# An embedding lookup on one core: the first indices move to a second issuing engine, and the second half of the positions moves ahead of the raw indices

## The chip, the cores and the metric

The kernel runs on one core of one Trainium2 chip. The metric is the time of one execution on the device, in microseconds (us), as the median of several runs. A second number appears in the profiles: the span, from the first to the last recorded instruction of one profiled execution. The span is some microseconds shorter than the device time.

The engines that matter here are GpSimd (POOL in the profile), which issues the gathers; VectorE (DVE), which adds the positions; ScalarE (ACT), which in the kernel before issues every plain transfer and computes nothing; and SyncE (SP), which in the kernel before issues nothing. The transfers themselves are moved by 16 DMA engines that all issuing engines share. A `q` after an engine's name in the profile (ACTq, POOLq) marks what the engine's sequencer did: issue, wait, drain.

## The reference

```python
batch, seq_len, vocab_size, d_model = 32, 512, 50000, 512
token_embed = embedding_table[indices]          # 32 x 512 rows of 2 KB
return (token_embed + position_embed).astype(np.float32)
```

So 16384 rows of 2 KB (33.55 MB) are read from a table of 50000 rows at random places, a row of positions is added to each, and 33.55 MB are written. The positions are 1 MB in all, and the indices reach the kernel as 64-bit words.

## The kernel before

A position s of the sequence is written as s = 4p + k: p is one of 128 partitions, k runs from 0 to 3. One gather takes 128 rows, those of one batch entry b and one k, so that there are 32 x 4 = 128 gathers of 256 KB, numbered g in the order in which they are issued. For the first four batch entries the order takes k = 0 and 1 of all four entries first, and then k = 2 and 3.

There are four kinds of loads. `idx0` holds the indices of the first four batch entries, fetched in the layout that the gathers need: entry 0 by itself (4 KB in pieces of 32 bytes), entries 1 to 3 after it (12 KB). `idx_raw` holds all indices as they lie in memory, in four loads of 32 KB, and one transpose on VectorE makes `idx_t` of them for the other 28 entries. The positions come in two halves of 512 KB: half 0 is for k = 0 and 1, half 1 for k = 2 and 3.

```python
    def load(out, in_, done):
        return nc.scalar.dma_start(out=out, in_=in_).then_inc(done, 16)      # L95

    def load_pos(h):
        part = slice(h * half, (h + 1) * half)
        return load(pos_sb[:, part, :], pos_rows[:, part, :], s_pos[h])

    # two loads ahead of the barrier with which the framework closes
    for ins in (load(idx0[:, 0, :], idx_first[:, 0, :], s_first), load_pos(0)):
        tc.no_tile_sem_insts.add(ins.ins.name)
    tc.close()                       # the profile gives the barriers to L106
    tc.compile()

    # the rest of the loads, behind the barrier
    load(idx0[:, 1:, :], idx_first[:, 1:, :], s_next)
    for j in range(J):               # J = 4
        load(idx_raw[j * B : (j + 1) * B, :], idx_rows[:, j, :], s_raw)
    load_pos(1)
```

GpSimd issues the gathers. It waits for entry 0's indices, for the next three entries' ahead of the third gather, and for the transpose ahead of the seventeenth:

```python
    nc.gpsimd.wait_ge(s_first, 16)
    for g, (b, k) in enumerate(order):
        if g == half:                # half = 2
            nc.gpsimd.wait_ge(s_next, 16)
        if g == FIRST * K:           # 16
            nc.gpsimd.wait_ge(s_idx, 1)
        # ... (a wait for stores, once, where the slots are reused)
        ins = nc.gpsimd.indirect_dma_start(                                  # L128
            out=slots[b % SLOTS][:, k, :], out_offset=None, in_=table,
            in_offset=bass.IndirectOffsetOnAxis(ap=where, axis=0),
        ).then_inc(s_gather[g % LANES], 16)
        if g >= LANES:               # 10 gathers may be under way
            ins._wait_ge(s_gather[g % LANES], rounds(g - LANES))
```

VectorE copies each quarter of the positions into PSUM when the first batch entry needs it, adds, and makes the transpose ahead of the eighth add:

```python
    for g, (b, k) in enumerate(order):
        if g == 7:
            nc.vector.transpose(out=idx_t[:], in_=...)._wait_ge(s_raw, 16 * J).then_inc(s_idx, 1)  # L140
        if b == 0:
            nc.vector.tensor_copy(out=pos_ps[:, k, :], in_=pos_sb[:, k, :])._wait_ge(              # L145
                s_pos[k // half], 16).then_inc(s_ps, 1)
            nc.vector.wait_ge(s_ps, k + 1)
        part = slots[b % SLOTS][:, k, :]
        nc.vector.tensor_tensor(out=part, in0=part, in1=pos_ps[:, k, :], op=add                    # L150
            )._wait_ge(s_gather[g % LANES], rounds(g)).then_inc(s_add, 1)
```

ScalarE then issues 68 stores (60 of 512 KB, 8 of 256 KB; L159), each as soon as the adds it needs are done. The last store's landing ends the kernel.

Of the kernel before, what the change touches and what calls it, by code (L numbers as in the profile page):

```python
# [1 line left out]

# [4 lines left out]

P = 128
K = 4
SLOTS = 23  # L10
LANES = 10
FIRST = 4
Q = 32


@with_exitstack
def kernel(
    ctx: ExitStack,
    tc: tile.TileContext,
    indices: bass.AP,  # L20
    embedding_table: bass.AP,
    position_embed: bass.AP,
    out: bass.AP,
):

    nc = tc.nc
    f32 = mybir.dt.float32
    i32 = mybir.dt.int32
    add = mybir.AluOpType.add

    B, S = indices.shape
    V, D = embedding_table.shape
    assert S == P * K and B == 32
    J = P // Q  # L40
    assert B == Q, "indices are turned in squares of 32"


    idx_words = indices.bitcast(i32)
    idx_first = idx_words[0:FIRST].rearrange("b (p w) -> p b w", p=P)
    idx_rows = idx_words.rearrange("b (j w) -> b j w", j=J)
    out_rows = out.rearrange("b (p k) d -> b p k d", k=K)
    pos_rows = position_embed.rearrange("(p k) d -> p k d", k=K)
    table = embedding_table[:, :]

    def sbuf(name, shape, dtype):
        return nc.alloc_sbuf_tensor(name, shape, dtype).ap()

    idx0 = sbuf("idx0", [P, FIRST, 2 * K], i32)
    idx_raw = sbuf("idx_raw", [P, 2 * Q * K], i32)
    idx_t = sbuf("idx_t", [P, K, B], i32)
    pos_sb = sbuf("pos_sb", [P, K, D], f32)
    slots = [sbuf(f"slot{n}", [P, K, D], f32) for n in range(SLOTS)]
    pos_ps = nc.alloc_psum_tensor("pos_ps", [P, K, D], f32).ap()

    half = K // 2
    order = [(b, k) for h in range(2) for b in range(FIRST)
             for k in range(h * half, (h + 1) * half)]
    order += [(b, k) for b in range(FIRST, B) for k in range(K)]
    stores = []
    for g, (b, k) in enumerate(order):
        if (b <= 1 and k < half) or b == B - 1:
            stores.append((g + 1, b, k, 1))  # L70
        elif k % half == half - 1:
            stores.append((g + 1, b, k + 1 - half, half))

    sems = []

    def sem(name):
        sems.append(nc.alloc_semaphore(name))
        return sems[-1]

    s_first, s_next, s_raw = sem("s_first"), sem("s_next"), sem("s_raw")  # L80
    s_pos = [sem(f"s_pos{h}") for h in range(2)]
    s_gather = [sem(f"s_gather{n}") for n in range(LANES)]

    reused = range(B - SLOTS)
    s_out, s_idx, s_ps = sem("s_out"), sem("s_idx"), sem("s_ps")
    s_add, s_rest, s_pool = sem("s_add"), sem("s_rest"), sem("s_pool")
    nums = [x.num for x in sems]
    assert nums == list(range(nums[0], nums[0] + len(nums)))
    early, late = range(nums[0], nums[-3]), range(nums[-3], nums[-1] + 1)

    def rounds(g):
        return 16 * (g // LANES + 1)

    def load(out, in_, done):
        return nc.scalar.dma_start(out=out, in_=in_).then_inc(done, 16)  # L95

    def load_pos(h):
        part = slice(h * half, (h + 1) * half)
        return load(pos_sb[:, part, :], pos_rows[:, part, :], s_pos[h])

    for ins in (load(idx0[:, 0, :], idx_first[:, 0, :], s_first), load_pos(0)):
        tc.no_tile_sem_insts.add(ins.ins.name)
    tc.close()
    tc.compile()  # L106


    load(idx0[:, 1:, :], idx_first[:, 1:, :], s_next)
    for j in range(J):  # L110
        load(idx_raw[j * B : (j + 1) * B, :], idx_rows[:, j, :], s_raw)
    load_pos(1)


    nc.gpsimd.wait_ge(s_first, 16)
    for g, (b, k) in enumerate(order):
        if g == half:
            nc.gpsimd.wait_ge(s_next, 16)
        if g == FIRST * K:
            nc.gpsimd.wait_ge(s_idx, 1)  # L120
        if b == SLOTS and k == 0:
            done = sum(1 for x in stores if x[1] in reused)
            nc.gpsimd.wait_ge(s_out, 16 * done)  # L123
        if b < FIRST:
            where = idx0[:, b, 2 * k : 2 * k + 1]
        else:
            where = idx_t[:, k, b : b + 1]
        ins = nc.gpsimd.indirect_dma_start(  # L128
            out=slots[b % SLOTS][:, k, :],
            out_offset=None,  # L130
            in_=table,
            in_offset=bass.IndirectOffsetOnAxis(ap=where, axis=0),
        ).then_inc(s_gather[g % LANES], 16)
        if g >= LANES:
# [5 lines that stand above are left out]
            nc.vector.transpose(  # L140
                out=idx_t[:],
                in_=idx_raw[:].rearrange("r (q k w) -> r k q w", k=K, w=2)[:, :, :, 0],
            )._wait_ge(s_raw, 16 * J).then_inc(s_idx, 1)
        if b == 0:
            nc.vector.tensor_copy(out=pos_ps[:, k, :], in_=pos_sb[:, k, :])._wait_ge(  # L145
                s_pos[k // half], 16
            ).then_inc(s_ps, 1)
            nc.vector.wait_ge(s_ps, k + 1)
        part = slots[b % SLOTS][:, k, :]
        nc.vector.tensor_tensor(  # L150
            out=part, in0=part, in1=pos_ps[:, k, :], op=add
        )._wait_ge(s_gather[g % LANES], rounds(g)).then_inc(s_add, 1)


    rest = 0
    for adds, b, at, n in stores:
        done = s_out if b in reused else s_rest
        rest += b not in reused
        nc.scalar.dma_start(  # L159
            out=out_rows[b][:, at : at + n, :],  # L160
            in_=slots[b % SLOTS][:, at : at + n, :],
        )._wait_ge(s_add, adds).then_inc(done, 16)

    nc.gpsimd.wait_ge(s_add, len(order))
    nc.gpsimd.drain()
    nc.gpsimd.dma_reset(early)
    nc.gpsimd.sem_clear(early).then_inc(s_pool, 1)
    nc.scalar.wait_ge(s_pool, 1)  # L170
    nc.scalar.wait_ge(s_rest, 16 * rest)
    nc.scalar.sem_clear(late)

# [1 line left out]
_INS = ['indices', 'embedding_table', 'position_embed']  # L175
_OUTS = [((32, 512, 512), 'float32')]


# [23 lines left out]
```

## Time and profile before

| | |
|---|---|
| device time, median of 3 runs | 179.27 us (178.99 to 179.32) |
| span of the profiled execution | 173.3 us |
| bytes moved in the span | 68.34 MB, 394 GB/s on average |
| VectorE busy | 90.7 us (52%) |
| GpSimd busy | 121.4 us (70%) |

The page of the profile also cuts the span into 40 slices of 4.3 us and gives, for each, the busy share of the 16 DMA engines and the rate. The rate is 128 and 242 GB/s in the first two slices, between 324 and 392 in the next five, and above 400 from the eighth slice to the last but one. A part of the page lists groups of instructions with their mean duration, and the idle time of the engine ahead of them with the name of what ended it; "issue" there means that the engine waited for nothing that the profile shows. A packet is a piece of a transfer that one DMA engine moves at a time. The trace has a record of each packet: its queue, size, start and duration. Queue q0 carries the gathers, and q10 carries everything that ScalarE issues.

### The profile page before, as it was taken

The page shows a single profiled execution, that of the slowest core. Times are in us where ns is not written, and L with a number is a line of the kernel's source. Part 1 is how long each engine was busy: PE and PEld are TensorE (multiplying, and loading weights), DVE is VectorE, ACT ScalarE, POOL GpSimd, SP SyncE. Part 2 cuts the span into 40 slices and gives each one's busy share as a digit, 9 for nine tenths or more (in the row PEclk, how much of TensorE's full clock was granted, in tenths as well). Part 3 has the DMA queues.
Part 4 walks back from the last instruction along what each step waited for, and adds up shares of the span by engine and source line. Part 5 has one row for each costly group of instructions (what it writes and reads, how often), then busy time and mean ns, then how long its engine had stood idle before and what let it go on. Part 6 is the DMA issues. An engine that isn't in the chain of part 4 may idle for free.

```text
span 173.3 us, 387 instructions
## 1 busy us (share of the span) xinstructions
DVE 90.7 (52%) x133; POOL 121.4 (70%) x132
## 2 busy tenths in 40 slices
DVE  0433855545555554555555555545555555546551
POOL 2777777777777777777777777777777777777400
DMA  4899999999999999999999999999999999999997
GB/s 128 242 324 331 345 392 365 415 409 412 411 415 402 407 421 419 409 421 420 420 416 421 420 417 419 422 416 420 421 419 417 421 419 418 419 422 415 420 420 308
DMA packets 21059, 68.34 MB, mean 394 GB/s; under 512 B 3776, under 2 KB 3904, under 8 KB 21056
## 3 DMA queue, kind: packets, MB, share of 16 engines
q10 hardware_dynamic: 10816, 34.76, 49.8%
q0 software_dynamic: 10240, 33.56, 49.7%
q14 instruction: 3, 0.02, 0.0%
HBM read 34.75 MB, written 33.55 MB: 394 GB/s over the span
## 4 chain that ended last, share of the span: by engine, by line
POOL 68%; issue 23%; DMA 5%; DVE 1%; POOLq 0%
POOL slot L128 68%; DMA slot<-in_embedding_table_dram,idx_t 4%; DVE slot L150 1%; DMA idx<-in_indices_dram 1%; POOLq L123 0%
## 5 line engine op out<-in xcount | busy, mean ns | idle before, releaser
L128 POOL DMA_INDIRECT slot<-in_embedding_table_dram,idx_t x112 | 105.9, 946 | 34.1 <-issue 34.1
L150 DVE TENSOR_TENSOR slot<-slot,pos_ps 128x512 f32<-128x512 f32 x128 | 87.9, 687 | 74.9 <-issue 46.1
L128 POOL DMA_INDIRECT slot<-in_embedding_table_dram,idx x16 | 15.3, 954 | 7.3 <-issue 4.6
L145 DVE COPY pos_ps<-pos_sb 128x512 f32<-128x512 f32 x4 | 2.8, 688 | 4.6 <-DMA pos_sb<-in_position_embed_dram 4.6
L140 DVE STREAM_TRANSPOSE idx_t<-idx_raw 128x128 int32<-128x128 int32 x1 | 0.4, 399 | 0.0
L186 POOL MEMSET const-float32-0.0<- 128x1 f32 x1 | 0.1, 98 | 0.2 <-issue 0.2
L186 POOL MEMSET const-uint8-127<- 128x1 uint8 x1 | 0.1, 118 | 0.0
L186 POOL MEMSET const-bfloat16-1.0<- 128x1 bf16 x1 | 0.1, 113 | 0.0
L186 POOL MEMSET const-float32-1.0<- 128x1 f32 x1 | 0.1, 104 | 0.0
## 6 DMA issues: line engine op xcount, KB each, us to landing
out_dram<-slot ACTq DMA_DIRECT2D x60, 512.0 KB
out_dram<-slot ACTq DMA_DIRECT2D x8, 256.0 KB
slot<-in_embedding_table_dram,idx_t POOLq DMA_INDIRECT x112
pos_sb<-in_position_embed_dram ACTq DMA_DIRECT2D x2, 512.0 KB, 4.6
slot<-in_embedding_table_dram,idx POOLq DMA_INDIRECT x16
idx_raw<-in_indices_dram ACTq DMA_DIRECT2D x4, 32.0 KB
idx<-in_indices_dram ACTq DMA_DIRECT2D x1, 4.0 KB, 1.6
idx<-in_indices_dram ACTq DMA_DIRECT2D x1, 12.0 KB
```

Of the source, the lines that this page charges most:

```text
L128: ins = nc.gpsimd.indirect_dma_start(out=slots[b % SLOTS][:, k, :], out_offset=None, in_=table, in_offset=bass.IndirectOffsetOnAxis(ap=whe ...
L140: nc.vector.transpose(out=idx_t[:], in_=idx_raw[:].rearrange("r (q k w) -> r k q w", k=K, w=2)[:, :, :, 0],)._wait_ge(s_raw, 16 * J).then_ ...
L145: nc.vector.tensor_copy(out=pos_ps[:, k, :], in_=pos_sb[:, k, :])._wait_ge(s_pos[k // half], 16).then_inc(s_ps, 1)
L150: nc.vector.tensor_tensor(out=part, in0=part, in1=pos_ps[:, k, :], op=add)._wait_ge(s_gather[g % LANES], rounds(g)).then_inc(s_add, 1)
L186: nc = _bacc.Bacc("TRN2", target_bir_lowering=False, num_devices=1)
```

## The change

The load of entry 0's indices is issued by SyncE, so that ScalarE can issue the first half of the positions at once, beside it. Behind the barrier, the second half of the positions is issued ahead of the four loads of raw indices and no longer behind them. The intent is to start the positions' two transfers earlier, in a stretch where few transfers are under way. No transfer is added or removed, and no wait of GpSimd, VectorE or of the stores is changed.

```diff
-    def load(out, in_, done):
-        return nc.scalar.dma_start(out=out, in_=in_).then_inc(done, 16)
+    def load(out, in_, done, engine=nc.scalar):
+        return engine.dma_start(out=out, in_=in_).then_inc(done, 16)
@@
-    for ins in (load(idx0[:, 0, :], idx_first[:, 0, :], s_first), load_pos(0)):
+    for ins in (
+        load(idx0[:, 0, :], idx_first[:, 0, :], s_first, engine=nc.sync),
+        load_pos(0),
+    ):
         tc.no_tile_sem_insts.add(ins.ins.name)
     tc.close()
     tc.compile()
 
     load(idx0[:, 1:, :], idx_first[:, 1:, :], s_next)
+    load_pos(1)
     for j in range(J):
         load(idx_raw[j * B : (j + 1) * B, :], idx_rows[:, j, :], s_raw)
-    load_pos(1)
```

## The prediction

> **What bounds the kernel now.** I read the chain of waits first, for what sets the end; then busy time in stretches, to see whether the DMA engines have room; then the timeline of the first 8 us, where the whole change lies; then the instructions of the barrier's line. The chain in order of time, cut to its first 8 us:
>
> ```profile
> 0.68 0.06 issue
> 0.74 1.60 DMA idx<-in_indices_dram
> 2.33 0.80 issue
> 3.13 1.08 POOL slot L128
> 4.21 0.31 issue
> 4.51 0.94 POOL slot L128
> 5.46 0.30 issue
> 5.76 0.95 POOL slot L128
> ```
>
> The columns are start, length and what it was. The chain is the load of entry 0's indices (1.60 us from issue to landing), 0.80 us in which nothing is named, and then gathers at a strict distance of 1.25 us (4.51, 5.76). The last of the 128 is issued at 162.06, and (162.06 - 4.51)/126 = 1.2504 us confirms that none was ever held up: 10 gathers may be under way, and the group of idle times says "issue" for 127 of 128. So GpSimd is a metronome, and the end is its start plus 127 x 1.25 plus the delay of the last gather, add and store. But the DMA engines are full too:
>
> ```profile
> 2.00:4.00 2.00, 0.00 (x0) 0.87 (x1) 1.00 0.78 257
> 4.00:5.00 1.00, 0.36 (x1) 0.69 (x2) 1.00 0.66 112
> 5.00:6.00 1.00, 0.34 (x1) 0.70 (x2) 1.00 0.78 230
> 6.00:8.00 2.00, 1.19 (x2) 1.65 (x2) 1.00 0.94 286
> ...
> 15.00:20.00 5.00, 2.98 (x6) 3.78 (x5) 1.00 1.00 360
> ...
> 100.00:160.00 60.00, 32.79 (x48) 45.37 (x49) 1.00 1.03 419
> 160.00:169.00 9.00, 5.01 (x8) 2.40 (x3) 1.00 1.03 419
> ```
>
> The last two columns are the share of the DMA engines and GB/s. From 6 us on the share is near 1. GpSimd asks for one gather and, later, one equal store in each 1.25 us: 2 x 262144 B / 1.2504 us = 419 GB/s, which is just what the engines move between 100 and 160 us, and also between 160 and 169, when GpSimd has stopped asking (its last issue ends at 163.0). Demand and capacity are therefore equal within what I can read. The backlog tells the same: from a gather's issue to its add the first takes 6.81 - 3.13 = 3.7 us, the last 169.54 - 162.06 = 7.5 us. What matters at the end is a sum of three: when gathers start, how much backlog the first 30 us leave, and the tail after the last gather's landing (173.3 - 169.5 = 3.8 us).
>
> What ends the wait of GpSimd at 3.13 is the point in doubt. The timeline of the loads and the barrier's line:
>
> ```profile
> 0.74 0.38 ACTq L95 DMA_DIRECT2D idx<-in_indices_dram  x1
> 1.15 0.46 ACTq L95 DMA_DIRECT2D pos_sb<-in_position_embed_dram  x1
> 2.36 0.39 ACTq L95 DMA_DIRECT2D idx<-in_indices_dram  x1
> 2.78 1.93 ACTq L95 DMA_DIRECT2D idx_raw<-in_indices_dram  x4
> 4.73 0.45 ACTq L95 DMA_DIRECT2D pos_sb<-in_position_embed_dram  x1
> ```
> ```profile
> L106 POOLq EVENT_SEMAPHORE  x4: 17/17/17, 1.8 to 2.2; - x4
> L106 ACTq DRAIN  x2: 8/80/151, 1.6 to 2.0; - x2
> ```
>
> ScalarE ends its second issue at 1.61, drains for 0.15 us, and only then does GpSimd's semaphore step of the barrier run (1.8); the other engines had drained by 0.8. ScalarE is the last to arrive, so its two issues set the barrier. GpSimd leaves it at 2.23 + 0.02 = 2.25; the indices land at 2.33. Two candidates thus lie 0.08 us apart, and either could be what the 0.80 us follow.
>
> [...] The trace puts that issue time at 0.38 to 0.46 us each[...]. [...] No two plain rings are at work together in the trace before, so it shows nothing of SyncE's; where gathers and raw indices overlap (5 to 6.4 us) the packet records show the 1 KB packets strewn among the gathers' 4 KB packets up to 6.37[...]. [...]
>
> **The change part by part.**
>
> Part one, the indices on SyncE. It takes one issue, 0.41 us (1.15 - 0.74), from ScalarE ahead of the barrier. SyncE is ready when ScalarE is: both leave the earlier barrier at 0.66 and SyncE's first drain of L106 is at 0.7. The best case: both issue at about 0.74, the indices land at 2.33 as before, half 0 of the positions starts 0.41 earlier, the barrier opens at 1.84 and everything that ScalarE issues behind it moves up 0.41. If the 0.80 us follow the barrier, the first gather still can't be ahead of the landing at 2.33 but may start near 2.72 (3.13 - 0.41). If they follow the landing, it stays at 3.13.
>
> The cost of part one is company. In the kernel before, the 128 packets of 32 B (7 to 9 ns each) run alone, from 1.73 to 1.99 by the packet records, and the positions' first 4 KB packet starts at 2.24. That is 0.99 and 1.09 us after their issues. With both issued at 0.74 the positions' packets begin at 1.83, within the indices' 0.26 us. Each DMA engine has 8 index packets; some 3 are through by 1.83 (8 x 0.10/0.26), and if the other 5 have to take turns with 4 KB packets of 160 to 500 ns each, they end 5 x 0.2 = 1.0 us later. [...] I weigh: no delay 45%, about half a microsecond 35%, near one microsecond 20%. Of the gain of 0.41 I take half, and of a delay that falls on GpSimd's start I count all: 0.5 x -0.41 x 0.45 + 0.35 x 0.45 + 0.2 x 0.9 = +0.25 us as a mean, with a median at 0 to +0.1.
>
> Part two, half 1 of the positions ahead of the raw indices. Its issue moves from 4.73 to about 2.37 (2.78 - 0.41), and the four raw loads from 2.78 to about 2.83, almost where they were. Nobody waits for either: the copy of quarter 2 runs at 19.2, and the transpose that reads the raw indices at 18.15, with no idle time ahead of it; its result is first used at 23.27. So no wait is removed. What changes is which packets fill the stretch from 4 to 6 us. There the engines move 0.112 + 0.230 = 0.34 MB; with 512 KB of positions in the queue they can move as much as in the stretches beside it, 257 to 286 GB/s, 0.54 MB in two microseconds. That takes 0.20 MB out of the full stretch, worth 0.20 MB / 419 GB/s = 0.48 us of backlog. The second gather and the ones after it lose the half load in front of them (the second took 10.28 - 4.51 = 5.8 us to its add); the first one gets it instead, and may land about half a microsecond later (4 of its packets on each engine, each behind one of 160 ns: 0.6 us). Moving everything of ScalarE up by 0.41 fills more of the same holes, up to another 0.2 us.
>
> How much of the 0.48 to 0.7 survives for 160 us is a choice. If capacity truly equals demand, a backlog that is smaller at 30 us is smaller at the end, and all of it counts. If instead the rate rises with the backlog (360 GB/s at 15 to 20 us, 419 later), the queue refills to the same level and none of it counts. I take 60%, -0.36 us.
>
> Sum: +0.05 (median of part one) - 0.36 = -0.3, so 179.27 - 0.3 = 179.0; the chance that the barrier is what GpSimd follows pulls a little further: 178.9 us.
>
> **The rivals.** First, the metronome alone: the end follows GpSimd's start and nothing else. For it speaks that no gather was held up. Then the time is 179.27 minus 0.41 if the barrier frees GpSimd (178.9), unchanged if the landing does, and up to 180.2 if the indices are slowed by 0.9 in company. Second, the DMA engines alone: GpSimd's start is of no matter, all work filled into holes counts. For it speaks the share of 1.03 after GpSimd has stopped, at 419 GB/s. Then 0.5 to 1.1 us are won: 178.2 to 178.8. Third, a second plain ring costs time that lies outside the span, at the program's start or end (179.27 against 173.3 us of span leaves 6 us that no view shows); nothing here speaks for or against it, and I allow half a microsecond.
>
> **Range and chances.** The extremes are -1.3 (the gains of both in full) and +1.0 (indices late, backlog refills); 8 times in 10 it should lie between 177.9 and 179.9. Two per cent are 3.6 us, more than all that the change touches in the first 6 us. I give 0.02 to faster by over 2%, 0.96 to within 2%, 0.02 to slower.
>
> **What would show it.** In the changed kernel's trace: ScalarE's first issue is the positions' at 0.74 and its next at about 1.95; SyncE's issue stands at 0.73 to 0.74, and its landing at 2.33 says that company is free, [...]at 3.2 or later that packets took turns. The first gather at 2.72 says barrier, at 3.13 landing. The stretch from 4 to 6 us should show 250 GB/s or more. The last gather's delay to its add, 7.5 us before, should be near 7.1 if the emptier queue survives, and 7.5 if it refills. The prediction is wrong if the indices land after 3.5, if the metronome of 1.25 us breaks because the next three entries' indices come late (needed at 5.76), or if the time moves by over 1 us with a span that doesn't.

## The result, and the profile after

The changed kernel took 177.92 us (median of 4 runs, 177.83 to 178.63) against 179.29 us before (4 runs): a ratio of 0.9936 with a 95% interval of 0.9908 to 0.9964. The span of the profiled execution hardly moved: 173.2 us after, 173.3 us before. So of the 1.37 us won in time, 0.1 us stands in the profile. One number on record bears on this at once: the execution of the kernel before whose span was 173.3 us took 177.92 us itself, which is the changed kernel's median. The kernel before thus stands on record at 177.92 us and at 178.99 to 179.32 us, without the change. That contradiction is the first thing to settle.

The chain of waits of the changed kernel, in order of time (start, length, what):

```profile
0.68 0.07 issue
0.74 2.08 DMA idx<-in_indices_dram
2.82 0.27 issue
3.09 1.08 POOL slot L131
4.17 0.30 issue
4.48 0.95 POOL slot L131
```

The load of the first indices now takes 2.08 us to land, 0.48 us more than before (1.60). But the unnamed stretch behind it shrank from 0.80 to 0.27 us, so that the first gather starts at 3.09, 0.04 us earlier than before. An "issue" piece that changes its length when its supposed cause moves was not caused by it. The barrier's line tells what was:

```profile
L109 POOLq EVENT_SEMAPHORE  x4: 17/17/17, 1.4 to 1.8; - x4
L109 ACTq DRAIN  x2: 8/80/153, 1.2 to 1.6; - x2
```

GpSimd's last step of the barrier moved from 2.2 to 1.8 (in the trace it ends at 2.25 before and at 1.79 after), behind a drain of ScalarE that starts 0.47 us earlier. The timeline of the loads shows why:

```profile
0.74 0.40 ACTq L95 DMA_DIRECT2D pos_sb<-in_position_embed_dram  x1
0.74 0.37 SPq L95 DMA_DIRECT2D idx<-in_indices_dram  x1
1.90 0.39 ACTq L95 DMA_DIRECT2D idx<-in_indices_dram  x1
2.32 0.51 ACTq L95 DMA_DIRECT2D pos_sb<-in_position_embed_dram  x1
2.86 1.87 ACTq L95 DMA_DIRECT2D idx_raw<-in_indices_dram  x4
```

Both engines issue at 0.74, and neither issue is longer than it was before (0.46 and 0.38). Last, the stretches (busy times, then the last two columns: share of the DMA engines, GB/s):

```profile
4.00:5.00 1.00, 0.69 (x1) 0.69 (x2) 1.00 0.79 242
5.00:6.00 1.00, 0.00 (x0) 0.70 (x2) 1.00 0.84 245
...
10.00:15.00 5.00, 2.41 (x4) 3.78 (x5) 1.00 0.85 245
15.00:20.00 5.00, 2.48 (x5) 3.78 (x5) 1.00 1.01 360
...
100.00:160.00 60.00, 32.79 (x48) 45.37 (x49) 1.00 1.03 419
```

and one stretch of the kernel before:

```profile
10.00:15.00 5.00, 2.70 (x5) 3.78 (x5) 1.00 0.99 346
```

The hole from 4 to 6 us is filled as intended: 242 and 245 GB/s where there were 112 and 230. But a new hole follows it: from 10 to 15 us the engines carry 245 GB/s where they carried 346. By the packet records the changed kernel is 0.23 MB ahead at 6 us, level at 12 us and 0.18 MB behind at 15 us. Nearly all that is missing from 10 to 15 us is gathers (0.64 against 1.11 MB; stores 0.59 against 0.61), and their 4 KB packets took 277 ns each on average, against 195 before and 159 from 100 to 105 us in both kernels. Why the packets take longer there isn't shown. So nothing is left at 15 us, and the last gather takes 169.62 - 162.02 = 7.6 us from issue to add, against 7.5 us before.

### The profile page after: what moved, and what is told of

Read it like the earlier page. It is cut to its first block, busy times and chain, and to the rows that moved or that the text cites. A ratio compares the mean times of both kernels' runs of the same rounds, so it can differ in the third digit from the quotient of the medians.

```text
span 173.2 us, 387 instructions
## 1 busy us (share of the span) xinstructions
DVE 90.4 (52%) x133; POOL 121.4 (70%) x132
## 4 chain that ended last, share of the span: by engine, by line
POOL 68%; issue 23%; DMA 5%; DVE 1%; POOLq 0%
POOL slot L131 68%; DMA slot<-in_embedding_table_dram,idx_t 4%; DMA idx<-in_indices_dram 1%; DVE slot L153 1%; POOLq L126 0%
```

## The experiments

They ran in three sets on three chips, the four kernels of a set on one chip, each beside the kernel before. Which chip the first measurement had isn't recorded. A span without further words is that of the profiled execution; a median of spans is over all executions of a run. The ratios and their intervals are those on record; a ratio is not the quotient of the two medians and can differ from it by 0.2%.

**Is the gain there again, and which part has it?** Four kernels: the kernel before (no edit), the changed kernel (no edit), and each part alone.

```diff
# part one alone: from the changed kernel
     load(idx0[:, 1:, :], idx_first[:, 1:, :], s_next)
-    load_pos(1)
     for j in range(J):
         load(idx_raw[...], idx_rows[:, j, :], s_raw)
+    load_pos(1)
# part two alone: from the kernel before
     load(idx0[:, 1:, :], idx_first[:, 1:, :], s_next)
+    load_pos(1)
     for j in range(J):
         load(idx_raw[...], idx_rows[:, j, :], s_raw)
-    load_pos(1)
```

> The kernel before against itself, to learn how far two sets of runs of one program differ. Theory A (the gain of the change is real and lies outside the span): ratio 1.000 within 0.2%, time about 179.3 us, span 173.3. Rival (before has two levels of its own, 177.9 and 179.3 us, and the change moves nothing): the runs scatter between 177.9 and 179.3 us with one and the same span.

> The changed kernel again. Theory A: about 177.9 us, 0.7% under before, with a span of 173.2 us as before. Rival: the ratio comes nearer to 1.000 than 0.998, as the spans (173.2 against 173.3 us) say.

> Only the load of the first indices goes to SyncE; the second half of the positions stays behind the raw indices. If the gain comes with the second ring or with the shorter way to the barrier, the time is that of the changed kernel, about 177.9 us. If the gain is from the order of the loads, it is 179.3. In the trace the indices land at about 2.8 us in both cases, slowed by the positions beside them, and the first gather starts near 3.1.

> Only the order of the loads behind the barrier changes; ScalarE issues all. If the holes in the first 6 us are what was won, the time falls by 0.5 us or more. If the queue refills to the same level (a last gather that takes 7.5 us from issue to add), the span stays at 173.3 us and the time at 179.3. The indices land at 2.33, the first gather starts at 3.13.

| | time, us | ratio to before, 95% interval | median span, us | first gather, us |
|---|---|---|---|---|
| before, again | 175.14 | 1.0009 (0.9991 to 1.0027) | 173.7 | 3.13 |
| changed, again | 175.40 | 1.0010 (0.9994 to 1.0026) | 173.95 | 3.31 |
| part one alone | 175.12 | 1.0004 (0.9989 to 1.0020) | 173.65 | 3.27 |
| part two alone | 175.47 | 1.0022 (1.0005 to 1.0040) | 174.0 | 3.13 (third: 6.48) |

The gain isn't there again. The kernel before is 4.2 us shorter here while its span is not: the time is the span plus 1.47 us (medians 1.46 to 1.47 in these four). In the first measurement it was the span plus 4.7 to 5.3 us in the four executions of the changed kernel, and plus 4.6 us in the one profiled execution of the kernel before. My theory A, a real gain outside the span, fell; its rival for the changed kernel held. The rival for the kernel before expected two levels at one span. In this run they were not seen; but the record of the kernel before from the first measurement holds both, 177.92 us in the profiled execution and 178.99 to 179.32 us in the four others.

Part two alone costs something, and its chain shows what, a few lines that end at the third gather:

```profile
2.29 0.06 issue
2.35 3.86 DMA idx<-in_indices_dram
6.22 0.26 issue
6.48 0.94 POOL slot L128
```

The indices of entries 1 to 3 now have half 1's 4 KB packets right behind them and take 3.86 us to land, at 6.22; before they landed at 4.73. The third gather was due at 5.76 and comes at 6.48. I had not thought that a load could be slowed by one issued after it on its own ring (in the trace, a queue: q10 for all that ScalarE issues, q1 for SyncE's load). The changed kernel shows the same (5.57, against 4.62 with part one alone); its third gather, at 5.95, was not yet held up by it.

**The first indices alone.** The same load on SyncE, with nothing of ScalarE's ahead of the barrier:

```diff
     for ins in (
         load(idx0[:, 0, :], idx_first[:, 0, :], s_first, engine=nc.sync),
-        load_pos(0),
     ):
@@
     load(idx0[:, 1:, :], idx_first[:, 1:, :], s_next)
+    load_pos(0)
     load_pos(1)
```

> The first indices on SyncE as in the changed kernel, but ScalarE issues nothing ahead of the barrier: entries 1 to 3's indices come first behind it, then half 0, half 1, the raw indices. Theory (GpSimd is free 0.88 us after the barrier and 0.27 us after the landing, whichever is later, and the end follows it): the indices land at 2.33 us again, the barrier opens near 1.8, the first gather starts at 2.65 to 2.70 and the span is 0.4 to 0.5 us under that of the kernel before. Rival (the DMA engines bound it, GpSimd's start is of no matter): half 0 of the positions comes 1.1 us later than in the changed kernel, which leaves a hole in the first 4 us, and the time is the same or longer.

```profile
0.74 1.57 DMA idx<-in_indices_dram
2.31 0.36 issue
2.68 1.08 POOL slot L131
```

The landing is back at 2.31, the barrier ends for GpSimd at 1.80, and the first gather starts at 2.68, which is 0.88 us after the barrier. That is the very distance of the kernel before (3.13 - 2.25 = 0.88). Where the landing comes late, the distance from it is 0.27 us in all seven executions profiled with half 0 beside the indices and no further wait. So the first gather starts 0.88 us after the barrier or 0.27 us after the landing of the indices, whichever is later. Time: 174.80 us, ratio 0.9991 (0.9975 to 1.0007); median span 173.35 us against 173.8 for the kernel before on that chip, 0.45 us less, as the theory had it, while the interval of the ratio doesn't exclude 1.000.

**Bytes at the start, bytes in the middle.** Three runs ask whether the DMA engines' queue keeps what it gains or loses. One leaves half 1 of the positions out (k = 2 and 3 then add half 0), one fetches it twice at the start, one fetches it again, from SyncE, after 64 adds:

```diff
# less, from the changed kernel
-    load_pos(1)
-            nc.vector.tensor_copy(out=pos_ps[:, k, :], in_=pos_sb[:, k, :])._wait_ge(
-                s_pos[k // half], 16
+            nc.vector.tensor_copy(out=pos_ps[:, k, :], in_=pos_sb[:, k % half, :])._wait_ge(
+                s_pos[0], 16
# more (here and in mid, without the lines that reserve `spare` and wait for it at the end)
     load_pos(1)
+    load(spare[:], pos_rows[:, half:, :], s_spare)
# mid
+    nc.sync.dma_start(out=spare[:], in_=pos_rows[:, half:, :])._wait_ge(
+        s_add, 64).then_inc(s_spare, 16)
```

> The changed kernel without half 1 of the positions: k = 2 and 3 add half 0 again, so this leaves out 512 KB of loads and its output has other numbers in these places. If the DMA engines bound the whole kernel, 0.52 MB at 419 GB/s is 1.25 us less. If the queue refills to one level behind a GpSimd that keeps its 1.25 us, the time is that of the changed kernel within 0.2 us and the last gather takes 7.5 to 8 us from issue to add as ever.

> The changed kernel with half 1 of the positions fetched a second time, to a place that nobody reads, right behind the first: 512 KB more in the first 10 us. Bound by the DMA engines: 1.25 us longer. Queue that settles to one level: no change beyond 0.3 us.

> The changed kernel with the same 512 KB fetched from SyncE when 64 adds are done, in the middle of the steady stretch. If capacity is just the demand of 419 GB/s, the extra 0.52 MB stays in the queues to the end: 1.25 us longer, and gathers from then on take about 1 us longer. If there is room above 419 GB/s, the delay of the gathers rises after 86 us and falls back to 7.5, and the time doesn't change.

Less: ratio 1.0006 (0.9987 to 1.0025), within noise of the changed kernel's 1.0010, with half a megabyte less to move. More: 1.0025 (1.0003 to 1.0047), some 0.3 us above the changed kernel, and up to 0.65 us by its interval; 0.1 us of it is a third gather at 6.04 in place of 5.94. A whole megabyte lies between these two runs on one chip. At 419 GB/s it would be 2.5 us; the ratios differ by 0.3 us, the median spans (173.6 and 174.1) by 0.5 us. Mid: 1.0098 (1.0075 to 1.0120), a median span of 175.15 us, 1.35 us above the kernel before beside it. Stretches of the run with less:

```profile
6.00:30.00 24.00, 13.30 (x21) 18.21 (x20) 1.00 0.95 324
30.00:40.00 10.00, 5.14 (x8) 7.56 (x9) 1.00 1.02 381
40.00:160.00 120.00, 65.31 (x96) 90.74 (x97) 1.00 1.03 418
```

and of the run with more:

```profile
6.00:30.00 24.00, 12.95 (x21) 18.17 (x20) 1.00 0.98 352
30.00:40.00 10.00, 5.48 (x9) 7.56 (x9) 1.00 1.02 408
40.00:160.00 120.00, 65.48 (x96) 90.71 (x97) 1.00 1.03 418
```

From 6 to 30 us the engines carry 324 or 352 GB/s, at shares of 0.95 and 0.98: a share near 1 did not mean that no more could be moved. From 40 us on both carry 418, and the last gather takes 7.65 and 7.4 us to its add. In the middle there is no such room. The end of the chain of the run with the load at 90 us:

```profile
162.25 9.06 DMA slot<-in_embedding_table_dram,idx_t
171.31 0.02 issue
171.33 0.69 DVE slot L155
```

A gather took 7.1 to 7.8 us to its add from 50 to 87 us (ahead of the extra load, which is issued at 90.2) and 8.4 to 9.2 us from 88 us to the end. The median rose from 7.45 to 8.7 us, by the 1.25 us that 0.52 MB take at 419 GB/s. The theory that says "there is room above 419 GB/s" fell, the one that says a queue at 7.5 us keeps every byte held; at the start bytes cost little.

**Repeats, and a late start.** The first indices alone but issued by ScalarE; the kernel with them alone once more; the changed kernel a third time; and the changed kernel with one more wait:

```diff
# alone, by ScalarE
-        load(idx0[:, 0, :], idx_first[:, 0, :], s_first, engine=nc.sync),
+        load(idx0[:, 0, :], idx_first[:, 0, :], s_first),
# late, from the changed kernel
     nc.gpsimd.wait_ge(s_first, 16)
+    nc.gpsimd.wait_ge(s_pos[0], 16)
```

> As the run with the first indices alone ahead of the barrier, but ScalarE issues them and SyncE issues nothing. Theory (what counts is that the 32 B pieces have no company and that one issue only stands ahead of the barrier; the second ring is of no use): indices at 2.33 us, first gather at 2.60 to 2.70, span 0.4 to 0.5 us under the kernel before if a gather takes 1.250 us again. Rival (SyncE's ring is what helped): the first gather is at 3.1 as before.

> The same kernel as the run with the first indices alone on SyncE, once more. There each gather took 1.2533 us from issue to issue, where all other kernels had 1.2500 to 1.2506, which cost 0.37 us of the 0.45 us won at the start. If that belongs to the kernel, the step is 1.253 again and the last gather is issued near 161.97; if it belonged to the one execution, the step is 1.250 and the last gather is issued near 161.55, 0.45 us ahead of the kernel before.

> The changed kernel a third time. Theory (nothing is won inside the span; the 0.6% of the first measurement lay outside it): ratio within 0.3% of 1.000, and a time that is the span plus one constant in all runs. Rival (won, and missed once by chance): ratio 0.994.

> The changed kernel with GpSimd waiting for half 0 of the positions too, ahead of its first gather. That holds the first gather back by about 1.1 us, to 4.3 or 4.4 us, and nothing else. If the end follows GpSimd's start, the span is about 1.1 us longer than that of the changed kernel. If the DMA engines bound it by the bytes alone, the positions fill the time and less than 0.5 us is lost.

| | time, us | ratio to before, 95% interval | median span, us | first gather, us |
|---|---|---|---|---|
| alone, by ScalarE | 174.99 | 0.9999 (0.9982 to 1.0016) | 173.55 | 2.68 |
| alone, by SyncE, again | 174.86 | 0.9988 (0.9974 to 1.0002) | 173.4 | 2.67 |
| changed, third time | 175.52 | 1.0019 (1.0005 to 1.0034) | 174.05 | 3.29 |
| late | 176.91 | 1.0118 (1.0084 to 1.0151) | 175.45 | 5.02 |

With ScalarE issuing them the first gather starts at 2.68 too, so a second ring isn't needed for that. The changed kernel is 0.2% slower than before, not 0.6% faster. The kernel with the first indices alone is the better of the two on this chip, 174.86 against 175.52 us, a median span 0.65 us shorter; against the kernel before its intervals still reach 1.000. Late missed its own number: GpSimd started 0.9 us after half 0 had landed (4.13), not 0.27, so that the start moved by 1.73 us; the median span moved by 1.40. Why this second wait costs more than the first is open. Over these runs the end follows the start of the gathers, but only roughly one for one: against the kernel before, the start moved by -0.45 us with the first indices alone and the median span by -0.15 to -0.45, in the changed kernel by +0.16 to +0.18 and +0.35.

The step between gathers was 1.2526 us by ScalarE, 1.2524 again and 1.2528 in the changed kernel here, against 1.2498 and 1.2503 in the changed kernel earlier. All four executions profiled on this chip have the longer step, and one of four on the chip of the set before. So the longer step, 0.3 us over a whole run, doesn't belong to the changed kernel, which has shown both; what it is stays open.

The delay from a gather's issue to its add differs between executions too. Its median from 40 us on is 7.4 us in the changed kernel's first profile and 8.1 and 8.0 in its repeats; with the first indices alone on SyncE it is 7.4 and 8.1. This spread, as large as what the change was meant to win, is no kernel's own either, and it comes on top of any effect read from one profile.

## Why the prediction was right or wrong

The number held at the edge of its range (177.92 us in 177.9 to 179.9), and by luck: two later comparisons put the change at +0.10% and +0.19%, where the prediction had -0.2%. One of its own signs of being wrong, a time that moves by over 1 us with a span that doesn't, came true (1.37 us and 0.1 us). Its reasons fared as follows.

**Company of the indices: the step that was weighed wrongly.** I gave "no delay" 45%. The indices were late in every execution profiled beside half 0: they landed at 2.82 in the first and at 3.00 to 3.04 in the seven later ones, and at 2.31 to 2.41 when alone. The delay, 0.5 to 0.7 us, lies between my two branches, about half a microsecond and near one; the first was my estimate, and no trace had shown a reason for it. The packet records say how. Beside its data the load has 16 packets of 4 bytes, and its semaphore rises in 16 steps: in the kernel before those packets ran from 1.80 to 2.00 and the steps from 2.10 to 2.33. In the first execution of the changed kernel the 128 data packets ended at 2.04, nearly as before (1.99), but the 16 small packets ran from 2.01 to 2.47, beside half 0's 4 KB packets, which ran from 1.80 on; the steps went from 2.33 to 2.82. In the seven later ones the data themselves ended only at 2.55 to 2.59, which is most of the delay, and the small packets at 2.71 to 2.75. In the changed kernel's first repeat, 56 index packets ran by 1.87 and the other 72 from 2.19 to 2.58: a pause of 0.3 us, and then all of them. My 1.0 us was an estimate of five turns of 0.2 us each, with a turn for each 32-byte piece and 8 pieces on each DMA engine (128 over 16; the records name no engine). The record shows the one pause in their place. Why the small packets of the first execution came late where its data did not isn't shown.

**Barrier or landing: left open, now settled.** In the kernel before it was the barrier (0.88 us ahead of the first gather), and the landing had 0.80 - 0.27 = 0.53 us of slack. The change opens the barrier 0.46 us earlier (predicted 0.41) and delays the landing by as much or more, so one limit took the place of the other: the first gather moved by -0.04 us in the first profile and by +0.14 to +0.18 in the repeats. Without the delay it would be at 2.68.

**The two issues: side by side.** SyncE's and ScalarE's issues ran side by side in 0.37 and 0.40 us; one after the other on ScalarE, the same two loads took 0.38 and 0.46. Their first packets started at 1.71 and 1.80, 0.97 and 1.06 us after the issues (0.99 and 1.09 before). The measurement shows no waiting of one for the other.

**Half 1 earlier: the hole filled, and nothing was won.** It filled to 242 and 245 GB/s (I asked for 250). The first gather paid more for it than I had worked out: 8.44 - 3.09 = 5.35 us to its add against 3.7, where I had 0.6 us more; the fourth add started at 11.04, ahead of 12.71. The failed step is "60% of the emptier queue survives", -0.36 us. The lead of 0.23 MB at 6 us was a lag of 0.18 MB at 15, in the first repeat as well (from +0.21 to -0.28 MB, with 234 GB/s from 10 to 15 us against 311). And a whole megabyte more or less in the first 10 us moved the time by 0.3 to 0.5 us in place of 2.5. The sign that I had named, a last gather at 7.1 or at 7.5 us, can't decide it: in three executions of the changed kernel that delay was 7.6, 8.1 and 8.0 us.

**The metronome held** (1.2503 us a gather), and with it, roughly, the first rival, the end that follows GpSimd's start. The second rival, bytes alone, fell at the start and held at 90 us, the one later place where it was tried.

**Outside the span: undersized, and the only place left for the first result.** I allowed half a microsecond there. The 6 us that I read there came from the time of some executions and the span of another, which took 177.92 us and so leaves 4.6. The first measurement's 1.37 us has 0.1 us in the span of the profiled executions; the rest must lie outside or in executions of the kernel before whose spans aren't recorded. Since the kernel before reached 177.92 us without the change, a difference of this size can arise without it. Two repeats on two chips, where time minus span is a constant 1.5 us, show no gain. Why the first measurement had it stays open; that the second ring is the cause isn't shown, and part one alone (1.0004) speaks against it.

## What to carry to other kernels

Ahead of the first dependent work, try giving the small load that everything waits for the DMA engines to itself: a large load issued beside it on another ring saved 0.46 us at the barrier and cost 0.5 to 0.7 us in the landing. Before filling a hole in the DMA stretch, ask in which stretch a byte costs time (here about 0.2 us for 512 KB at the start and over 1 us in the middle), and look at the stretches behind the hole too. And when time and span disagree, compare the time and the span of one and the same execution, and measure again before explaining the time.

## What the runs showed of the hardware that was not expected

A load landed later when a larger one was issued behind it on the same ring: entries 1 to 3's indices landed at 4.73 with the raw indices behind them and at 6.22 with 512 KB of positions behind them, though they were issued near 2.35 in both. In these runs GpSimd started its first gather no sooner than 0.88 us after the barrier and 0.27 us after the landing of its indices; with a second wait behind that one, it was 0.9 us after the second landing. The step of the gathers had two values, 1.250 and 1.253 us, and the median delay from a gather to its add lay between 7.3 and 8.4 us in executions without the load at 90 us; one and the same kernel showed both ends of the step, and delays of 7.4 and 8.1. And a DMA share near 1 stood beside 324 and beside 418 GB/s (0.95 and 1.03).
